# A planner that counts TensorE's instruction blocks, two products in other PSUM banks, and 25 stretches of the program with other priorities

## The chip, the cores and the metric

The kernel runs on one core of a Trainium2 chip. The metric is device time in microseconds (us) of one execution. Three runs of the kernel before gave 710.45 to 711.79 us, with a median of 711.58 us. One further execution was recorded by the hardware profiler, and all views below are of that one. Engines are named as the profile names them: PE is TensorE's matmuls, PEld its weight loads, DVE is VectorE, ACT is ScalarE, POOL is GpSimd, and SP is SyncE, which issues most DMAs.

## The reference

One layer of a decoder trunk over 512 tokens of width 1024, all in f32. Three groups of heads read the same normed input through one projection; their outputs are joined and go through one output projection; then comes a dense SwiGLU.

```python
h = rmsnorm(x, norm_mix[l])
mem_h = rmsnorm(mem, norm_mem[l])
proj = h @ w_in[l]
c_q, c_kv, k_rope, hq, hf, hi, hg, mq = [proj[..., offsets[j]:offsets[j + 1]] for j in range(len(IN_SIZES))]
y_mla = mla_group(c_q, c_kv, k_rope, positions, q_a_norm[l], w_uq[l], kv_a_norm[l], w_ukv[l],
                  mla_q_norm[l], mla_k_norm[l])
y_hg = hgrn2_group(hq, hf, hi, hg, lb_all[l], hg_out_norm[l])
y_mem = mem_group(mq, mem_h, w_mem_kv[l], mem_q_norm[l], mem_k_norm[l])
mix = jnp.concatenate([rmsnorm(y_mla, mla_out_norm[l]), y_hg, rmsnorm(y_mem, mem_out_norm[l])], axis=-1)
x = x + (mix @ w_out[l]).astype(x.dtype)
h2 = rmsnorm(x, norm_ffn[l])
x = x + ((jax.nn.silu(h2 @ w_gate[l]) * (h2 @ w_up[l])) @ w_down[l]).astype(x.dtype)
```

The first group is attention with low-rank q and kv, a rotary key and a causal softmax, the third is cross-attention into 256 memory tokens; each group has four heads. In the recurrence each head has q, k, v and a forget gate f per token: the state is multiplied by f, k's outer product with v is added, and q reads the state out.

## The kernel before, in words

**Arithmetic.** Nearly all products run on PE in the fp32r format. An f32 operand is split into a high part (`wh`, `xh`, `hd`: rounded by a copy) and a low part (`wl`, `xl`: source minus high part, on DVE), and `mm3` issues three matmuls, high by high, high by low and low by high, into one PSUM bank. `split`, `piece` and `pieces` make the two parts of a weight; `load` issues the weight's DMA on SP into a buffer `wr`.

**Planner.** `body` doesn't issue instructions. It calls a `Recorder`, which gives every operation a number in the order of the code (there are 5539), finds what it depends on, and gives it a price in ns (`price`) and a priority: its number plus a million times a class (0 for splits, evictions and loads, 1 as a rule, 2 for most projections). `base` adds two million from the FFN on. `run` then plays the five queues in time. At each step it takes, on the engine that can start first, the ready operation with the lowest priority number; an operation that needs a new tile waits until a buffer of that tag is free, and tiles of a tag are given out in the order of the code. Some operations may go to another engine than the code names when the planner finds them done sooner there (`others`). The order that comes out is issued as it stands, so each engine executes its part of it strictly in that order. The line numbers in the profile are therefore those of the two issuing lines: L383 for all operations, L380 for groups of small matmuls (`tiles`).

**PSUM.** There are eight banks under three tags: `mm` (3), `at` (3), `tr` (2). `gated` makes one 128-feature block of a projection: `feat` accumulates 8 x 3 matmuls into a bank, and DVE then multiplies it by `RX`, the per-token scale of the input's RMSNorm, into an SBUF tile `td`. `RX` exists only once the input's sums of squares are through. The first two blocks (i = 5 and i = 9: the first head's q and forget gate) have their weights under `in_we` and are multiplied chunk by chunk as `x` arrives. All blocks of `gated` take a bank `mm`.

**Stages, in the order of the code.** `hg_in`: eight blocks for the recurrence's q and f. `wide`: its values (weights `wva`, matmuls of 320 columns, and `wvb`, of 256 columns). `hg_levels`: inside chunks of 32 tokens, each level takes scores of all four heads by one `tiles` operation of 64 small f32 matmuls (32 x 32 columns; each becomes two passes, so 128 matmuls and 128 weight loads in the profile, `at<-y,tm`), DVE puts them in place under a mask (`put`, a copy_predicated), and `step_up` multiplies q, k and totals up to the next level, ten or more DVE operations. Then come `lowrank` (the compressed q and kv), the up projections (`wuq`, `wukv`), four heads of causal attention (`transposed`, `softmax`, `weights_t`, `pv`), the memory group, the output projection in two parts, and the FFN. The FFN runs in three column groups (`FF`), each with a gate and an up half made by `fast`, a scheme of seven block products (`prod`) instead of eight. `fast` loads weight blocks on SP (`get`) and adds further blocks onto them by accumulating DMAs on POOL (`more`), which must wait until the former content has been split. Each third ends with transposes of the activated product `ptl`, `p`, `qr`, `RX` and the `down` products.

**Price list.** The lines that the change touches: `price` for ACT (92 or 45 ns + 0.835 ns per element), for DVE's scalar_tensor_tensor (68 + 1.15 per element) and for DVE's other operations, copy_predicated among them (68 + 1.045). A `tiles` operation of 64 parts has the price 270 + 2.1 x 64 x 35 / 4 = 1446 ns, and nothing in the planner limits how soon the next one may follow.

Of the kernel before, what the change touches and what calls it, by code (L numbers as in the profile page):

```python
# [9 lines left out]
F32R = mybir.dt.float32r  # L10
I32 = mybir.dt.int32
U8 = mybir.dt.uint8
AF = mybir.ActivationFunctionType
# [33 lines left out]
class Recorder:  # L47
# [137 lines left out]
    def price(self, o, outs, ins):  # L185
        n = max(self._free(a) for a in outs)
        if o.name == "dma_start":
            return 1000 if o.eng == "gpsimd" else 475
        if o.eng == "tensor":
            if o.name == "tiles":  # L190
                return 270 + 2.1 * sum(max(35, self._free(p[2])) for p in o.kw["parts"]) / len({self._rng(p[0])[2] for p in o.kw["parts"]})
            if o.name == "transpose":
                return 109.5
            if ins[0].dtype == F32R:
                return n / 2.4 + (15.5 if n >= 512 else 14) if n >= 256 else max(1.67 * n, 107)
            return 222 if n <= 2 else 64 if n <= 32 else 122 if n <= 64 else 226 if n <= 128 else 436 if n <= 256 else 1.7 * n
        m = max([self._free(a) for a in ins] + [n])
        fast = self.inside(ins)
        if o.eng == "scalar":
            fn = o.args[2] if o.name == "activation" else None  # L200
            if fn is not None:
                o.table = self.TABLES.get(str(fn).split(".")[-1])
            return (92 if fast else 45) + 0.835 * m + (190 if "accum_out" in o.kw else 0) + (100 if hasattr(o.kw.get("scale"), "ap") else 0)
        if o.eng == "vector":
            if o.name == "reciprocal":
                return 70 + 6.6 * m
            if o.name == "tensor_copy":
                return 66 + (0.55 if fast else 1.045) * m
            if o.name == "tensor_scalar":
                return 66 + (0.62 if fast else 1.045) * m + 60 * any(hasattr(a, "ap") for a in o.args[2:])  # L210
            if o.name == "memset":
                return 60 + 0.5 * m
            if o.name == "scalar_tensor_tensor":
                return 68 + 1.15 * m
            return 68 + 1.045 * m
        if o.name == "memset":
            return 40 + m * 0.8
        if o.name == "tensor_scalar":
            return 244 + 0.84 * m
        return 170 + 2.17 * m  # L220
# [16 lines left out]
    }  # L237


    IDLE = (1500, 3400)  # L240

    def run(self):
        ops = self.ops
        for o in ops:
            o.left = len(o.preds)
            o.ready = 0.0
            for p in o.preds:
                ops[p].succs.append(o.n)
# [12 lines left out]
                    cand[e].append(o)  # L261
        table, dma, done, out, port, cold = None, 0.0, 0, [], 0.0, 0.0
        busy = {e: 0.0 for e in engs}
        while done < len(ops):
            best = None
            for e in engs:
                be = None
                for o in cand[e]:
                    t = max(free[e], o.ready)
                    if o.alts[e][5]:  # L270
                        t = max(t, port)
                    ok = True
                    if o.new:
                        need = {}
                        for k in o.new:
# [12 lines left out]
                            t = max(t, sorted(free_)[skip + j])  # L288
# [3 lines left out]
                    t = max(t, free[e])  # L292
# [33 lines left out]
            if o.eng == "tensor":  # L326
                if t - free["tensor"] > self.IDLE[0] or not free["tensor"]:
                    cold = t + self.IDLE[1]
                slow = min(2 * cost, max(0.0, cold - t))
                cost += slow / 2  # L330
            end = t + cost
            if both:
                port = end
# [2 lines left out]
            if o.dma:  # L336
                ap = o.kw["out"]
# [71 lines left out]
def body(ctx, tc, t):  # L409
# [14 lines left out]
    def nm(p):  # L424
        cnt[0] += 1
        return f"{p}_{cnt[0]}"
# [6 lines left out]
    def sb(tag, shape=(P, S), dt=F32):  # L433
        return rec.tile("SB", shape, dt, tag, nm(tag), BUFS[tag])

    def ps(tag, bufs, shape=(P, S)):
        return rec.tile("PS", shape, F32, tag, nm(tag), bufs)

    def ps_mm():
        return ps("mm", BUFS["mm"])  # L440

    def ps_at():
        return ps("at", BUFS["at"])

    def ps_tr():
        return ps("tr", BUFS["tr"])
# [28 lines left out]
    with rec.first(0):  # L475

        o = rec.tile("PS", (P, S), F32, "tr", nm("tr"), BUFS["tr"])
# [17 lines left out]
    def load(src, n=1024):  # L495

        raw = sb("wr", (P, 1024))
        with rec.first(0):
            DMA.dma_start(out=raw[:, :n], in_=src)
        return raw  # L500
# [43 lines left out]
    def colsums(sqs, nblk=NB, more=None):  # L544

        o = ps_ts()[:, 0:2 * nblk * len(sqs)]
        ks = [(i, b) for i in range(len(sqs)) for b in range(nblk)]
        v = o.rearrange("p (i b two) -> p i b two", two=2, b=nblk)
        T.tiles(o, ones, *sqs, parts=[
            (v[g:g + 32, i, b], sqs[i][:, b * P + g:b * P + g + 32], ones, (i, b) == ks[0], (i, b) == ks[-1] and more is None)  # L550
            for i, b in ks for g in range(0, P, 32)
        ])
        if more is not None:
            T.tiles(o, ones, more, parts=[
                (v[g:g + 32, 0, b], more[:, b * P + g:b * P + g + 32], ones, False, b == nblk - 1)
                for b in range(nblk) for g in range(0, P, 32)
            ])
        return v[..., 0]
# [27 lines left out]
    with rec.first(0):  # L586
# [6 lines left out]
        for k in range(KD):  # L593

            if k in EARLY:
                n, tag = EARLY[k]
# [9 lines left out]
        for k in range(KD):  # L606
            if k in EARLY:
                n = EARLY[k][0]
# [15 lines left out]
    def feat(dst, raw, acts):  # L624

        if isinstance(raw, list):
            w = raw.__getitem__
        else:
            w = pieces(raw)
        for k in range(KD):  # L630
            mm3(dst, w(k), acts[k], k == 0, k == KD - 1)
# [68 lines left out]

    def gated(i):

        o = ps_mm()
        feat(o, early[i // 9] if i in (5, 9) else load(t["wf"][i]), xg)
        z = sb("td")
        s_ = sb("td")
        with rec.first(0):
            V.tensor_tensor(z, o, RX, ALU.mult)
            A.activation(s_, z, AF.Sigmoid)
        return z, s_  # L710

    def hg_in(h):
        with rec.first(2):
            z, s_ = gated(5 + h)
            q = f(spots.pop(0))
            with rec.first(0):
                V.scalar_tensor_tensor(q, z, 128 ** -0.5, s_, ALU.mult, ALU.mult)
            z, s_ = gated(9 + h)
            fg = f(spots.pop(0))
            k_ = sb("tm")  # L720
            with rec.first(0):
                A.activation(fg, s_, AF.Identity, bias=lb[:, h:h + 1], scale=omlb[:, h:h + 1])
                A.activation(k_, fg, AF.Identity, bias=ones[:, 0:1], scale=-1.0)
                V.tensor_scalar(fg, fg, 1.0, None, ALU.min)
        return q, k_, fg
# [145 lines left out]
    def hg_gate(h, y):  # L871
        with rec.first(2):
            z, s_ = gated(13 + h)
        V.tensor_tensor(z, z, s_, ALU.mult)
        V.tensor_tensor(y, y, z, ALU.mult)
# [65 lines left out]
    with rec.first(0):  # L941
        o = colsums([cq_sq, ckv_sq])
# [25 lines left out]
    for h in range(4):  # L968
        o = ps_mm()
# [11 lines left out]
    for b in range(NB):  # L981
        o = ps_mm()[:, :256]
# [3 lines left out]
        o = o.rearrange("p (h d) -> p h d", h=4)  # L986
# [44 lines left out]
    for i in range(2):  # L1031
        w = [piece(r, i * S, (i + 1) * S) for r in wukv]
        for b in range(NB):
            o = ps_mm()
# [69 lines left out]
    def rope_t(src):  # L1104

        o = ps_tr()
        for b in range(NB):
            T.transpose(o[:, b * P:(b + 1) * P], src[:, b].rearrange("p a b -> p (a b)"), ident)
        return o

    ym = []
    for h in range(4):
# [6 lines left out]
        if h % 2 == 0:  # L1119
            o = rope_t(qr[:, :, h:h + 2, :])  # L1120
# [12 lines left out]
        for g in range(2):  # L1133
            pb = []
            for b in (2 * g, 2 * g + 1):
# [3 lines left out]
                o = ps_at()  # L1139
# [34 lines left out]
    for h in range(4):  # L1174
        o = ps_mm()
# [19 lines left out]
    for h in range(4):  # L1195
# [6 lines left out]
        for g in range(2):  # L1202
            pb = []
            for b in (2 * g, 2 * g + 1):
                bs = slice(b * P, (b + 1) * P)
                o = ps_at()
# [9 lines left out]
    with rec.first(2):  # L1216
        for i in range(KD):
            y = sb("tm")
            DMA.dma_start(out=y, in_=t["xT"][:, i * S:(i + 1) * S])
            o = ps_mm()  # L1220
# [12 lines left out]
    o = ps_tr()  # L1233
# [7 lines left out]
    for i in X_ORDER:  # L1241
        o = ps_mm()
# [54 lines left out]
    o = ps_tr()  # L1297
# [101 lines left out]
    for c0, w in FF:  # L1399
# [16 lines left out]
        for j in range(2 * w // P):  # L1416
            g, js = (cu[0:2] + cu[4:6], j * P) if j < w // P else (cu[2:4] + cu[6:8], j * P - w)
            hi, lo = sb("mx" if last else "xh", dt=F32R), sb("y" if last else "xl", dt=F32R)
            with rec.first(0):
                o = ps_tr()  # L1420
# [100 lines left out]
```

## Time and profile before

| what | value |
|---|---|
| median of three runs | 711.58 us (710.45 to 711.79) |
| the profiled execution's own time | 709.22 us |
| its span, first to last instruction | 707.4 us |
| instructions in the profile | 12975 |
| DVE busy | 546.7 us (77%) |
| ACT busy | 375.3 us (53%) |
| POOL busy | 92.8 us (13%) |
| moved by DMA | 98.04 MB, 139 GB/s on the mean |

The profiled execution lies 2.4 us below the median of the runs, and 1.8 us of it lie outside the span. PE's busy time counts matmuls whose starts are pipelined: a matmul of 512 columns is shown with some 0.39 us, while the next one starts some 0.23 us after it. What tells of lost time on PE is the idle time before an instruction, which the views print in square brackets with the instruction that ended it; "issue" there is a wait that nothing in the profile explains.

### The profile page before, as it was taken

How to read it: one execution, taken by the hardware profiler on the slowest of the kernel's cores; microseconds unless marked ns; L12 is line 12 of the kernel's file. 1: busy time of each engine (PE TensorE's matmuls, PEld its weight loads, DVE VectorE, ACT ScalarE, POOL GpSimd, SP SyncE). 2: the span in 40 equal slices, each digit the busy share in tenths (PEclk: the TensorE clock that was granted, in tenths of full speed). 3: DMA queues.
4: the chain of work that ended last, by engine and by line, in shares of the span. 5: the costliest groups of instructions: out<-in, count | busy, mean ns of one | idle time of the engine just before them, and what ended most of it. 6: DMA issues, size and time to landing. Idle time of an engine off the chain costs nothing.

```text
span 707.4 us, 12975 instructions
## 1 busy us (share of the span) xinstructions
PE 688.6 (97%) x4755; PEld 574.1 (81%) x4755; DVE 546.7 (77%) x1234; ACT 375.3 (53%) x721; POOL 92.8 (13%) x124
## 2 busy tenths in 40 slices
PE   8998899999999999999999998999999999999997
PEld 6787877887888877887878786888888899999886
DVE  7986799779989989888999769656549767548732
ACT  7763245447587654664776553645543365544420
POOL 1000000000000000000323442023112312310000
PEclk9999999999999999999999999999999999999999
DMA  8522221113333323215999899779957848941251
GB/s 284 161 66 91 84 63 46 31 63 120 89 120 120 118 65 101 75 31 183 281 278 226 182 244 218 191 164 219 212 127 184 162 130 193 225 87 34 68 146 62
DMA packets 47727, 98.04 MB, mean 139 GB/s; under 512 B 5424, under 2 KB 15536, under 8 KB 47664
## 3 DMA queue, kind: packets, MB, share of 16 engines
q1 hardware_dynamic: 33408, 73.62, 32.3%
q0 software_dynamic: 13824, 23.07, 20.4%
q8 instruction: 37, 0.61, 0.3%
q10 hardware_dynamic: 432, 0.53, 0.2%
q14 instruction: 26, 0.21, 0.1%
HBM read 95.11 MB, written 2.10 MB: 137 GB/s over the span
## 4 chain that ended last, share of the span: by engine, by line
PE 86%; DVE 6%; issue 3%; DMA 3%; ACT 2%; ACTq 0%; POOL 0%; DVEq 0%; POOLq 0%
PE mm L383 43%; PE tr L383 21%; PE at L383 20%; DMA xl<-in_wg 2%; DVE wl L383 2%; PE at L380 1%; DMA tc<-in_we 1%; DVE hd L383 1%; PE tr L380 1%; ACT wh L383 0%; DVE ptl L383 0%; DVE td L383 0%; DVE qr L383 0%; ACT hd L383 0%; DVE tm L383 0%
## 5 line engine op out<-in xcount | busy, mean ns | idle before, releaser
L383 ACT CAST wh<-wr 128x512 fp32r<-128x512 f32 (+2 forms) x141 | 84.0, 599 | 101.0 <-PE tr L383 44.4
L383 DVE TENSOR_TENSOR wl<-wr,wh 128x512 fp32r<-128x512 f32 (+2 forms) x148 | 96.9, 658 | 33.9 <-issue 11.6
L383 PE MATMUL mm<-xh,wh 128*128 128x512 f32 x248 | 98.0, 398 | 2.0 <-DVE td L383 1.5
L383 PE MATMUL mm<-xh,wl 128*128 128x512 f32 x248 | 98.4, 397 | 0.0
L383 PE MATMUL mm<-xl,wh 128*128 128x512 f32 x248 | 98.1, 396 | 0.1
L383 DVE TENSOR_TENSOR wl<-y,wh 128x512 fp32r<-128x512 f32 (+1 forms) x84 | 53.4, 638 | 41.8 <-PE tr L383 19.3
L383 ACT CAST wh<-y 128x512 fp32r<-128x512 f32 (+1 forms) x82 | 47.4, 581 | 65.9 <-PE at L383 35.5
L383 DVE TENSOR_TENSOR wl<-mx,wh 128x512 fp32r<-128x512 f32 (+1 forms) x72 | 46.1, 645 | 33.5 <-PE tr L383 14.8
L383 PE MATMUL mm<-wh,hd 128*128 128x512 f32 (+2 forms) x176 | 59.7, 366 | 0.7 <-ACT wh L383 0.7
L383 ACT CAST wh<-mx 128x512 fp32r<-128x512 f32 (+1 forms) x67 | 39.0, 585 | 37.2 <-PE at L383 17.7
L383 PEld LDWEIGHTS mm<-xh,wh 128*128 128x128 f32 x248 | 46.6, 188 | 11.5 <-DVE td L383 1.8
L383 PEld LDWEIGHTS mm<-xl,wh 128*128 128x128 f32 x248 | 46.6, 188 | 9.9 <-DVE xl L383 1.0
L383 PEld LDWEIGHTS mm<-xh,wl 128*128 128x128 f32 x248 | 46.7, 188 | 9.0 <-DVE wl L383 0.4
L383 POOL DMA_DIRECT2D y<-in_wu x36 | 32.2, 955 | 104.4 <-DVE wl L383 77.2
L383 PE MATMUL at<-wh,hd 128*128 128x512 f32 (+1 forms) x120 | 45.0, 375 | 0.0
L383 PE MATMUL tr<-xl,wh 128*128 128x512 f32 x112 | 43.8, 391 | 0.0
L383 PE MATMUL tr<-xh,wl 128*128 128x512 f32 x112 | 43.7, 390 | 0.0
L383 PE MATMUL tr<-xh,wh 128*128 128x512 f32 x112 | 43.7, 390 | 0.0
L383 PEld LDWEIGHTS mm<-wh,hd 128*128 128x128 f32 x176 | 32.3, 188 | 5.8 <-ACT wh L383 1.1
L383 PE MATMUL mm<-wh,v 128*128 128x512 f32 (+1 forms) x96 | 35.8, 375 | 0.0
L383 PE MATMUL at<-wh,v 128*128 128x512 f32 (+1 forms) x96 | 35.8, 375 | 0.0
L383 PE MATMUL mm<-wl,hd 128*128 128x512 f32 (+2 forms) x88 | 32.5, 369 | 0.4 <-DVE wl L383 0.4
(409 smaller groups left out, 1676.9 us busy)
## 6 DMA issues: line engine op xcount, KB each, us to landing
wr<-in_wf SPq DMA_DIRECT2D x19, 512.0 KB, 3.4
wr<-in_wd SPq DMA_DIRECT2D x16, 512.0 KB, 4.7
mx<-in_wg SPq DMA_DIRECT2D x24, 256.0 KB, 5.4
mx<-in_wu SPq DMA_DIRECT2D x24, 256.0 KB, 5.7
y<-in_wu POOLq DMA_DIRECT2D x24, 256.0 KB, 6.3
tm<-in_xT SPq DMA_DIRECT2D x16, 256.0 KB, 4.5
wr<-in_wt SPq DMA_DIRECT2D x8, 512.0 KB, 3.8
wr<-in_wo SPq DMA_DIRECT2D x8, 512.0 KB, 3.6
```

What stands on the lines that cost most here:

```text
L380: r = self.nc.tensor.matmul(get(a), lhsT=get(b), rhs=get(c), start=first, stop=last, skip_group_check=True)
L383: r = getattr(getattr(self.nc, o.eng), o.name)(*[get(a) for a in o.args], **{k: get(a) for k, a in o.kw.items()})
```

## The change

It has three parts, all in the plan or in tile tags; no operation is added or taken away.

1. **Prices and a count of blocks in the planner.** ACT activations of the kind Identity cost 90 ns more, scalar_tensor_tensor with a tile as its scalar 35 ns more, copy_predicated 118 in place of 68 ns. New: `length` gives PE operations a number of instructions (2 for a transpose or an fp32r matmul, 4 for an f32 matmul, 4 per part of a `tiles` operation). `run` counts these, starting from 63, and at each multiple of 256 it does not let the new block begin earlier than 5200 ns after the one before; what is missing is added to the operation's price.
2. **Other banks for two products.** In `gated`, blocks 5 and 9 take a bank `at` and no longer a bank `mm`.
3. **25 stretches get other priorities.** `NUDGE` holds triples (first, last + 1, shift): the shift is added to the priority of these operations. A positive shift puts them behind more of the others that are ready.

Where the stretches lie, by operation number (counted in the order of the code):

| operations and shift | what they are |
|---|---|
| 381-384 +76, 415-437 +197, 447-450 +346, 448-451 -155, 526-527 +71 | `wide`: matmuls of `wva` and `wvb`, and the splits of one weight piece |
| 606-649 +233, 617-638 -329 | last value splits; the first four `tiles` operations of `hg_levels` and their DVE steps |
| 791-800 +36 | `lowrank`: matmuls of the first block |
| 1159-1170 +125, 1280-1281 +16 | `wuq` and `wukv` products |
| 1871-1917 -113 | end of the last causal head; first memory weights with 2 loads on SP |
| 2480-2481 +413, 2552-2576 -90, 2651-2672 +978, 2666-2678 -114 | output projection, first part: blocks with 2 loads on SP each |
| 2912-2915 -11, 2923-2937 +28 | FFN input: differences and splits |
| 3042-3061 +1406, 3078-3080 +75 | first gate half: products 1 and 5 with their splits |
| 3321-3355 -51, 3385-3478 +368, 3440-3442 -146, 3549-3551 +692 | first up half: products 5, 7, 6, 2, 4; 4 loads on SP, 8 on POOL |
| 3588-3685 -133 | first third's transposes; second gate half's loads (12 on SP, 12 on POOL) and first product |
| 5484-5497 +129 | `down` of the last third: one load, one output DMA, splits, matmuls |

```diff
@@ price
-            return (92 if fast else 45) + 0.835 * m + (190 if "accum_out" in o.kw else 0) + (100 if hasattr(o.kw.get("scale"), "ap") else 0)
+            return (92 if fast else 45) + 0.835 * m + 90 * (fn == AF.Identity) + (190 if "accum_out" in o.kw else 0) + (100 if hasattr(o.kw.get("scale"), "ap") else 0)
...
             if o.name == "scalar_tensor_tensor":
-                return 68 + 1.15 * m
+                return 68 + 1.15 * m + 35 * hasattr(o.args[2], "ap")
+            if o.name == "copy_predicated":
+                return 118 + 1.045 * m
             return 68 + 1.045 * m
@@ class Recorder
+    FETCH, BLOCK, AHEAD = 5200, 256, 63
+
+    def length(self, o):
+
+        if o.name == "tiles":
+            return 4 * len(o.kw["parts"])
+        return 2 if o.name == "transpose" or o.kw["rhs"].dtype == F32R else 4
...
+    NUDGE = ((1159, 1171, 125), (1871, 1918, -113), (2651, 2673, 978), (2666, 2679, -114), (2552, 2577, -90), (3042, 3062, 1406), (5484, 5498, 129), (2480, 2482, 413), (1280, 1282, 16), (526, 528, 71), (2912, 2916, -11), (3588, 3686, -133), (2923, 2938, 28), (3385, 3479, 368), (3078, 3081, 75), (3321, 3356, -51), (791, 801, 36), (3549, 3552, 692), (381, 385, 76), (3440, 3443, -146), (617, 639, -329), (415, 438, 197), (447, 451, 346), (448, 452, -155), (606, 650, 233),)
 
     def run(self):
         ops = self.ops
+        for a, b, d in self.NUDGE:
+            for o in ops[a:b]:
+                o.prio += d
...
         busy = {e: 0.0 for e in engs}
+        begun, count = -1e9, self.AHEAD
...
                 slow = min(2 * cost, max(0.0, cold - t))
                 cost += slow / 2
+                n, full = self.length(o), cost
+                count += n
+                for b in range((count - n) // self.BLOCK + 1, count // self.BLOCK + 1):
+                    at = t + cost - full * (count - self.BLOCK * b) / n
+                    cost += max(0.0, begun + self.FETCH - at)
+                    begun = max(at, begun + self.FETCH)
@@ gated
-        o = ps_mm()
+        o = ps_at() if i in (5, 9) else ps_mm()
         feat(o, early[i // 9] if i in (5, 9) else load(t["wf"][i]), xg)
```

## Prediction

> **What bounds the kernel now.** I read the page first: which engine is busy, at what clock, and who holds the chain that ended last.
>
> ```profile
> PE 688.6 (97%) x4755; PEld 574.1 (81%) x4755; DVE 546.7 (77%) x1234; ACT 375.3 (53%) x721; POOL 92.8 (13%) x124
> PEclk9999999999999999999999999999999999999999
> PE 86%; DVE 6%; issue 3%; DMA 3%; ACT 2%; ACTq 0%; POOL 0%; DVEq 0%; POOLq 0%
> ```
>
> PE is busy 97% of the span, at full clock in all slices, and holds 86% of the chain. The change neither adds nor removes a matmul, so it can gain only what PE idles, and it loses by any idle time that the new order brings. The second view is therefore PE's list of waits, which has 13 rows; here are the larger ones and the last.
>
> ```profile
> PE at L380 <- issue: 4.5, 2, 2.9
> PE tr L383 <- DVE ones_r L383: 2.0, 1, 2.0
> PE tr L383 <- DVE ptl L383: 2.0, 2, 1.7
> PE mm L383 <- DVE td L383: 1.5, 1, 1.5
> PE at L380 <- DVE tm L383: 1.1, 2, 0.8
> PE mm L383 <- ACT wh L383: 0.7, 1, 0.7
> PE mm L383 <- DVE wl L383: 0.7, 3, 0.3
> PE mm L383 <- ACT xh L383: 0.5, 2, 0.3
> ...
> PE tr L383 <- DVE kr L383: 0.2, 1, 0.2
> ```
>
> The columns are the total, the number of waits and the longest. The rows shown make 13.2 us; the four left out hold 0.3 or 0.4 us each, 1.4 us in sum. Of the whole, 14.6 us, the 2.0 us for `ones_r` lie before the first matmul and the 0.5 us for `xh` in the arrival of the input, which no part of the change touches. About **12.1 us** are all that a better order could gain: 1.7% of the time.
>
> **Part 2 of the change: banks for the first two blocks.** The timeline around 25 us (start, duration, instruction, idle time before it):
>
> ```profile
> 19.20 0.40 PE L383 MATMUL mm<-xh,wh 128*128 128x512 f32 x1
> 19.43 0.39 PE L383 MATMUL mm<-xl,wh 128*128 128x512 f32 x1
> ...
> 24.73 0.47 PE L383 MATMUL mm<-xh,wl 128*128 128x512 f32 x1
> 25.06 0.58 ACT L383 COPY RX<-tr 128x512 f32<-128x512 f32 x1
> 25.92 1.28 DVE L383 TENSOR_TENSOR td<-mm,RX 128x512 f32<-128x512 f32 x2
> 26.66 0.50 PE L383 MATMUL mm<-xh,wh 128*128 128x512 f32 x1 [1.46 <-DVE td L383]
> ```
>
> Blocks 5, 9 and the third one hold all three `mm` banks, and `RX` is ready only at 25.64, so the fourth block waits until DVE has drained the first bank. With blocks 5 and 9 in `at` banks, the fourth and fifth block find two `mm` banks free. What could be late next is the sixth block, two blocks of 24 matmuls later (24 x 0.23, the step between the first two rows, is 5.5 us each), by when the third bank is drained. The `at` banks are next wanted by the first score operation past 58 us. Bounds: nothing, if the fourth block's split weights are not ready (DVE makes one at 25.31 to 26.00), and 1.7 us with the refilling of the pipeline. I take **-1.5**, the row of the wait.
>
> **Part 1: blocks of instructions.** The wait "issue" of 4.5 us comes twice, both times inside a score operation:
>
> ```profile
> 60.64 0.86 PE L380 MATMUL at<-y,tm 128*32 128x32 f32 x76
> 64.39 0.65 PE L380 MATMUL at<-y,tm 128*32 128x32 f32 x52 [2.89 <-issue]
> 80.37 1.13 PE L380 MATMUL at<-y,tm 128*32 128x32 f32 x108
> 83.09 0.38 PE L380 MATMUL at<-y,tm 128*32 128x32 f32 x20 [1.59 <-issue]
> 88.27 1.30 PE L380 MATMUL at<-y,tm 128*32 128x32 f32 x128
> ```
>
> An undisturbed one (the last row) runs 128 matmuls and as many loads in 1.30 us. The page's queue list and the window from the stall's beginning to its end say what is fetched in that time:
>
> ```profile
> q8 instruction: 37, 0.61, 0.3%
> ...
> q8 instruction: 1, 0.02, 2.1%
> ```
>
> PE has 2 x 4755 = 9510 instructions; 9510 / 256 = 37.1, and queue 8 brought 37 packets: blocks of 256 instructions, one of which lands in the first stall. Counting 256 back from the second stall gives the pace that the chip keeps:
>
> ```profile
> 77.90:81.49 3.59, 3.59 (x129) 3.30 (x127) 2.44 (x7) 0.62 (x1) 0.00 (x0) 1.00 0.47 151
> ```
>
> 129 matmuls and 127 loads took 3.59 us, and with the stall of 1.59 they make 5.18 us. Before the first stall 256 instructions reach back to about 59.2 us: 2.3 us and 2.89 make again 5.2. So a block takes at least 5.2 us; the planner's new FETCH is this number, and its boundary can be checked by it. A score operation is itself 256 instructions in 1.3 us, and stalls when most of one falls into one block; where a boundary cuts it in the middle (the one at 88.27) the rest of the block, some 64 wide matmuls, lasts longer than 5.2 us by itself. The planner only has to move these operations by some matmuls of `wide`, which are there in plenty, and the first seven stretches do this. Bounds: nothing gained, if the count is off, and -4.5. I take **-4.2**, near the upper end, and leave 0.15 us each time.
>
> The Trainium skill (page "Runtime: NRT & Kernel Launch", section "Instruction fetch mechanics") also has refills in blocks of 256 instructions, but calls the cost of crossing a block mostly hidden and the fetch faster than PE's dispatch. By that rule the stalls would be something else and the term 0, the forecast 4.2 us higher. The two stalls above, with a block landing in the first, speak against it.
>
> **The scores' other waits.** The rest of the waits of score operations are on DVE's steps between levels.
>
> ```profile
> L380 PE MATMUL at<-y,tm 128*32 128x32 f32 x704 | 7.9, 198 | 5.3 <-issue 4.5 <-DVE tm L383 0.8
> 58.00:88.00 30.00, 25.29 (x654) 23.82 (x653) 22.52 (x59) 7.41 (x15) 0.00 (x0) 1.00 0.25 80
> 88.00:124.00 36.00, 34.53 (x509) 27.95 (x509) 33.28 (x105) 17.68 (x42) 0.00 (x0) 1.00 0.18 58
> L383 DVE COPY_PREDICATED tc<-lmask,at 128x512 f32<-128x512 uint8 x5 | 3.7, 740 | 7.4 <-PE at L380 7.4
> ```
>
> In the two windows the columns are PE, PEld, DVE, ACT and POOL busy. From 88 to 124 us PE idles 1.5 us and DVE only 2.7, so a chain of levels that starts later has little room; from 58 to 88 DVE idles 7.5 us. A copy_predicated takes 740 ns; the old price for 512 elements is 603, the new one 653: nearer, not there. The dearer Identity and scalar_tensor_tensor only correct the plan in the same sense and move no work that the trace shows waiting; I cost them at nothing. Of the waits here (1.1 us on `tm` in the list) I take half, **-0.6**; bounds -1.1 and +2.7, the latter if a delayed chain eats DVE's slack and PE pays as much again.
>
> **The FFN's first third.** Its largest wait is for the activated product:
>
> ```profile
> 436.20 0.39 PE L383 MATMUL at<-wh,hd 128*128 128x512 f32 x1
> 436.31 0.70 DVE L383 TENSOR_TENSOR ptl<-mm,ptl 128x512 f32<-128x512 f32 x1
> 437.51 1.42 DVE L383 SCALAR_TENSOR_TENSOR ptl<-ptl,r,tc 128x512 f32<-128x512 f32 x2
> 438.32 0.44 PE L383 MATMUL tr<-cst,ptl 128*128 128x128 f32 x2 [1.74 <-DVE ptl L383]
> ...
> 380.00:400.00 20.00, 19.79 (x115) 15.18 (x115) 19.22 (x42) 13.06 (x21) 5.75 (x7) 1.00 0.91 201
> 400.00:420.00 20.00, 20.00 (x89) 16.27 (x88) 11.81 (x20) 11.03 (x21) 4.39 (x6) 1.00 1.04 251
> 420.00:440.00 20.00, 17.45 (x76) 12.91 (x76) 19.08 (x31) 6.78 (x12) 8.03 (x10) 1.00 1.03 232
> ```
>
> DVE idles 8.2 us between 400 and 420 and 0.9 us in the next 20, where PE idles 2.6; ACT idles 13.2 us there. The last products end, and four DVE operations stand between them and the transposes, while the next third's weights queue for the same DVE. The stretches from 3042 to 3685 reorder these products, splits and loads; the same work fits without the wait if a product or splits move ahead. PE's waits here are `ptl` 2.0, `wh` 0.7 and `wl` 0.7, in sum 3.4. I take **-2.1**, some six tenths, since four DVE operations at the end remain in series; bounds -3.4 and +1.5 (DVE is full from 380 to 400, too).
>
> **The other stretches** (`lowrank`, `wuq`, attention, output projection, `down`) lie where PE's waits are 0.2 to 0.4 us each. I take 0, bounds -1 and +1. The loads moved there are 7 on SP and one output DMA. They are the cheapest to hide:
>
> ```profile
> SPq L383 <- DVE wl L383: 543.5, 162, 22.8
> y<-in_wu POOLq DMA_DIRECT2D x24, 256.0 KB, 6.3
> POOL y L383 <- DVE wl L383: 129.4, 29, 20.1
> ```
>
> SP spends 543.5 us in waits for DVE to release a buffer: buffers, not SP's order, set when loads start, so a load moved within SP's queue still goes out when a `wl` is done. The accumulating loads on POOL (20 moved, with 16 of SP, in the FFN stretches) also wait for DVE, and land 6.3 us after issue; two products of 24 matmuls, 11 us, hide that today.
>
> **Sum.** -1.5 - 4.2 - 0.6 - 2.1 = -8.4 us. The profiled execution would come from 709.22 to 700.8. The median of the runs is 2.36 us above that execution; the prediction is for the median: 711.58 - 8.4 = **703.2 us**, with its own range from 701 to 706.
>
> **Rivals.**
> *Everything goes.* The reordering also fills the small waits: 711.58 - 12.1 = 699.5 us. For it: the waits are spread over stages with stretches in them. Against it: DVE is full around most of them.
> *The count misses.* The planner's boundary lies elsewhere than the chip's (PE's own semaphore instructions are not in its count), or the stalls have another cause than blocks, and they stay or move to another score operation: 703.2 + 4.2 = 707.4 us. For it: 76 and 108 matmuls into an operation, a shift of some 50 matmuls decides. Against it: 9510 / 256 gives the 37 packets, so few instructions are uncounted, and two stalls of different length give one pace, 5.2 us. The Trainium skill's rule named above would lead to this time as well.
> *Late weights in the FFN: slower.* The up half's stretch +368 puts 4 SP and 4 POOL loads behind later products, and the stretch -133 draws 12 and 12 of the next gate half into the middle of them. If an accumulating load is issued only when its product is next, PE stands for its landing and the two steps of its split, 6.3 + 0.7 + 0.7 = 7.7 us (each step taken as long as the DVE operation at 436.31). One such load leaves the kernel 0.7 us faster; from two on it is slower: 711.58 - 8.4 + 15.4 = 718.6 us. Against it: today no accumulating load shows in PE's waits, and 11 us of products lie between.
>
> **How the numbers follow.** Forecast 0.56, everything goes 0.13, the count misses 0.21, late weights 0.10 (0.06 with two or more, 0.04 with one). About 0.2%, 1.4 us, is what a measurement of this kernel can tell from no change. Faster by more has the first two cases and nearly all of the third (707.4 is 4.2 below before), 0.88; one late load gives most of "same", 0.06; slower 0.06. The range for 8 in 10: down to 699.5, where everything goes; up to 708.8, the third case with 1.4 us of the unknown bounds on top.
>
> **What would show it.** The wait "issue" of L380 gone from PE's list, and score operations cut by block boundaries; no wait for `td` near 25 us; the wait for `ptl` near 436 below 1 us; DVE less idle between 400 and 420. Wrong would be: a DMA as the releaser of a PE wait in the FFN, a longer wait for `tm` between 88 and 124, or a stall "issue" at another place.

## The result and the profile after

The changed kernel takes **699.15 us** (median of 4 runs, 698.81 to 699.73); beside it the kernel before took 711.68 us (4 runs, 710.45 to 712.3). The ratio is 0.9826, with an interval of 0.9811 to 0.9842: 12.5 us faster. The forecast was 8.4 us and 703.2 us; the result lies just below the range, whose low end was 699.5.

The page of the changed kernel, the lines that answer to those of before:

```profile
PE 688.4 (99%) x4755; PEld 575.6 (83%) x4755; DVE 549.4 (79%) x1231; ACT 375.9 (54%) x723; POOL 93.8 (13%) x127
PEclk9999999999999999999999999999999999999999
PE 89%; DVE 8%; ACT 1%; issue 1%; DVEq 0%; ACTq 0%
```

PE's work is the same to 0.2 us; its idle time went. The complete list of PE's waits in the changed kernel (total, number, longest; the issuing lines 380 and 383 are now 405 and 408):

```profile
PE tr L408 <- DVE ones_r L408: 2.0, 1, 2.0
PE at L408 <- DVE tm L408: 0.6, 2, 0.4
PE tr L408 <- ACT tm L408: 0.6, 1, 0.6
PE at L405 <- DVE tm L408: 0.4, 1, 0.4
PE mm L408 <- DVE wl L408: 0.4, 2, 0.2
PE at L408 <- ACT p L408: 0.2, 1, 0.2
PE at L408 <- ACT tc L408: 0.2, 1, 0.2
```

The sum is 4.4 us against 14.6 before. "issue", `td`, `ptl` and `wh` are gone, and no DMA has come in as a releaser. The windows say in which stage the time was won. The columns are the length of the window, then the busy time of PE, PEld, DVE, ACT and POOL, PE's granted clock, the DMA share and GB/s. First the kernel before, then the changed one:

```profile
10.00:50.00 40.00, 38.49 (x199) 30.70 (x198) 37.10 (x97) 30.98 (x51) 0.00 (x0) 1.00 0.48 159
50.00:100.00 50.00, 45.29 (x1021) 41.30 (x1020) 38.98 (x106) 16.30 (x34) 0.00 (x0) 1.00 0.24 76
100.00:300.00 200.00, 197.33 (x1543) 161.82 (x1542) 177.68 (x494) 119.40 (x257) 4.38 (x16) 1.00 0.27 86
300.00:500.00 200.00, 196.53 (x978) 157.97 (x977) 162.33 (x312) 115.39 (x210) 52.24 (x61) 1.00 0.82 203
```

```profile
10.00:50.00 40.00, 39.98 (x208) 32.45 (x207) 37.99 (x99) 33.87 (x55) 0.00 (x0) 1.00 0.49 160
50.00:100.00 50.00, 49.37 (x1101) 44.77 (x1100) 43.38 (x122) 21.09 (x43) 0.00 (x0) 1.00 0.28 84
100.00:300.00 200.00, 198.17 (x1503) 161.34 (x1489) 175.79 (x482) 117.56 (x260) 6.39 (x20) 1.00 0.27 84
300.00:500.00 200.00, 199.64 (x995) 162.38 (x994) 168.08 (x314) 116.26 (x205) 53.61 (x62) 1.00 0.88 213
```

The first number less the second is PE's idle time: 1.5, 4.7, 2.7 and 3.5 us before, 0.0, 0.6, 1.8 and 0.4 after. So 1.5 us were won at the banks, 4.1 from 50 to 100 us, where most of the scores lie, 0.8 from 100 to 300 us and 3.1 in the last window, most of it in the FFN; with 0.5 us in the first 10 us, this is the 9.9 us by which the span became shorter (707.4 to 697.5). Cut at 125 us, the 0.8 us fall to the last scores: PE idles 1.5 us from 100 to 125 before and 0.5 after, and from 125 to 300 us 1.2 before and 1.3 after. The medians differ by 12.5. Some **2.5 us** of the gain stand in neither of these two profiles, and this is what the prediction missed most.

### The profile page after: what moved, and what is told of

It reads as the page before. It is cut to its first block, busy times and chain, and to the rows that moved or that the text cites. A ratio compares the mean times of both kernels' runs of the same rounds, so it can differ in the third digit from the quotient of the medians.

```text
span 697.5 us, 13013 instructions
## 1 busy us (share of the span) xinstructions
PE 688.4 (99%) x4755; PEld 575.6 (83%) x4755; DVE 549.4 (79%) x1231; ACT 375.9 (54%) x723; POOL 93.8 (13%) x127
## 4 chain that ended last, share of the span: by engine, by line
PE 89%; DVE 8%; ACT 1%; issue 1%; DVEq 0%; ACTq 0%
PE mm L408 43%; PE at L408 23%; PE tr L408 22%; DVE wl L408 2%; DVE tm L408 1%; DVE hd L408 1%; PE at L405 1%; DVE y L408 1%; DVE td L408 1%; DVE tc L408 1%; PE tr L405 1%; ACT wh L408 0%; DVE qr L408 0%; DVE sm L408 0%; ACT td L408 0%
## 5 line engine op out<-in xcount | busy, mean ns | idle before, releaser
L408 ACT CAST wh<-wr 128x512 fp32r<-128x512 f32 (+2 forms) x139 | 82.3, 595 | 85.7 <-PE mm L408 40.3
L408 PE MATMUL mm<-xh,wh 128*128 128x512 f32 x232 | 91.5, 396 | 0.0
L408 PE MATMUL mm<-xl,wh 128*128 128x512 f32 x232 | 91.4, 397 | 0.0
L408 PE MATMUL mm<-xh,wl 128*128 128x512 f32 x232 | 90.6, 395 | 0.2 <-DVE wl L408 0.2
L408 PEld LDWEIGHTS mm<-xh,wl 128*128 128x128 f32 x232 | 43.6, 188 | 8.7 <-DVE wl L408 0.6
L408 PEld LDWEIGHTS mm<-xh,wh 128*128 128x128 f32 x232 | 43.6, 188 | 8.4 <-ACT wh L408 0.2
L408 PEld LDWEIGHTS mm<-xl,wh 128*128 128x128 f32 x232 | 43.5, 188 | 8.3 <-DVE xl L408 0.2
```

Source lines behind the costliest of these rows:

```text
L408: r = getattr(getattr(self.nc, o.eng), o.name)(*[get(a) for a in o.args], **{k: get(a) for k, a in o.kw.items()})
```

## The experiments

The theory at first was the prediction's: counting blocks keeps the scores apart, and the stretches of the FFN take its wait away. The rival: the order comes from the stretches alone, wherever they lie. Four kernels leave out stretches from the changed kernel; prices, count and banks stay. No kernel has the prices alone.

**All stretches out.**

```diff
-    NUDGE = ((1159, 1171, 125), (1871, 1918, -113), (2651, 2673, 978), ...
+    NUDGE = ()
```

> The changed kernel without its 25 stretches: banks, prices and the count of blocks stay. Theory A (the prediction's): the count by itself makes the planner hold the score operations apart, so the two stalls 'issue' (4.5 us) and the wait for RX (1.5 us) go and the FFN's waits (3.4 us) stay: about 6 us below before, 705 to 707 us. Theory B: the planner takes the first ready operation and the count only tells it that it will have to wait; then stalls 'issue' of 4 us or more stay in the list of waits, only the 1.5 us of the banks is gained, and the time is 709 to 713 us.

Measured: 706.78 us (7 runs, 705.19 to 708.73), ratio 0.9935 (0.9912 to 0.9958). From PE's waits:

```profile
PE at L405 <- issue: 3.2, 1, 3.2
PE tr L408 <- DVE ptl L408: 2.4, 2, 2.2
...
PE at L405 <- DVE tm L408: 1.1, 2, 0.8
```

The time alone would speak for theory A, the list speaks for B as to the first stall: the count is in this kernel's plan, and a stall of 3.2 us remains. The planner only adds the missing time to the price of an operation: it sees the stall and pays it, since it always takes what can start first. The second stall is gone without any stretch, and the banks are not the reason, since the kernel with the banks alone (below) still has it. What is left is the count or the prices. The planner can be played through without the chip: with the count and the old prices it gives PE the order of the kernel before, past both stalls; with the new prices and no count it gives the order of this kernel there. So the order that goes with the loss of the second stall comes from the prices. This is computed, not measured.

**Groups of stretches out.** `no_early` drops the seven below operation 700, `no_mid` those from 791 to 2678, `no_late` those from 2912 on.

> The changed kernel without the seven stretches below operation 700 (values projection and scores). Theory A: as the changed kernel, 699 to 700 us, for the count does the work there. Theory B: stalls 'issue' return, 4 to 5 us, 703 to 705 us, while the FFN's wait for ptl stays away.

> The changed kernel without the stretches from 791 to 2678 (low-rank, attention, output projection). Prediction's view: they lie where PE waits little, so within 1 us of the changed kernel. Rival: they decide when the FFN's loads and splits start, or where blocks of instructions fall near 150 us, and 3 us or more come back as PE waits (ptl, or issue).

> The changed kernel without the stretches from 2912 on (FFN). Prediction's view: the FFN's waits of 3.4 us come back (ptl near 436 us of before, wh, wl), 702 to 703 us. Rival: the FFN's waits were set by how the stage is entered, and the time stays within 1.4 us of the changed kernel's 699.15.

Measured: without the early ones 703.89 us (701.82 to 704.34), ratio 0.9892 (0.9867 to 0.9916); without the middle ones 704.49 us (703.96 to 705.13), 0.9905 (0.9884 to 0.9927); without the late ones 700.15 us (700.04 to 700.43), 0.9844 (0.9819 to 0.987). The three single losses, 4.7, 5.3 and 1.0 us, make more than the 7.6 us of all together. Half-clock time, of which below, is in the first two and in the 7.6; but in the executions whose mean clock was nearest to full (0.999 without the early ones and with all out, 1.000 for the other two) the losses are 2.7, 4.9 and 1.0 us against 6.6 together, so the groups do not simply add.

PE's matmuls around 58 us without the early stretches (start, duration, instruction, idle time before it), then the same place in the changed kernel:

```profile
57.98 0.46 PE L405 MATMUL at<-ptl,tm 128*32 128x32 f32 x32
59.14 0.86 PE L405 MATMUL at<-y,tm 128*32 128x32 f32 x76
62.71 0.96 PE L405 MATMUL at<-y,tm 128*32 128x32 f32 x52 [2.70 <-issue]
```

```profile
57.18 0.46 PE L405 MATMUL at<-ptl,tm 128*32 128x32 f32 x32
57.56 0.42 PE L408 MATMUL tr<-wl,xh 128*128 128x320 f32 x1
...
60.74 0.31 PE L408 MATMUL tr<-wl,xh 128*128 128x320 f32 x1
60.98 1.30 PE L405 MATMUL at<-y,tm 128*32 128x32 f32 x128
```

Two `tiles` operations of 256 instructions follow each other here. Without the early stretches the second begins 0.7 us after the end of the first; in the changed kernel 22 matmuls of `wide` with 320 columns lie between them, 3.3 us, where the kernel before has 5. So the early stretches took the first stall away. Without the middle stretches nothing shows as "issue"; the largest waits are these:

```profile
PE mm L408 <- DVE wl L408: 1.9, 3, 1.4
PE mm L408 <- DVE qr L408: 1.2, 1, 1.2
PE at L405 <- DVE tm L408: 1.0, 2, 0.7
PE tr L408 <- DVE xl L408: 0.8, 1, 0.8
```

PE then idles 4.0 us between 300 and 500 us: 1.4 us near 388, 1.6 us near 429, where the first third ends, and 0.8 us near 452. Without the late stretches it idles 1.4 us there, against 0.4 us in the changed kernel. The wait for `ptl` itself comes back in none of the three kernels, only with all stretches out (2.4 us); without the middle ones waits for `qr` and `wl` stand in its place. So with the other stretches in, those between the scores and the FFN are worth 3.6 us of idle time here, and those that reorder the FFN's own products, to which the prediction gave it, 1.0 us.

**The count taken out, the stretches left in.**

```diff
-    FETCH, BLOCK, AHEAD = 5200, 256, 63
+    FETCH, BLOCK, AHEAD = 0, 256, 63
```

> The changed kernel with all stretches, banks and prices, but the least time of a block set from 5200 ns to 0, so that the planner no longer sees blocks. Theory 'the stretches carry the gain': they keep the score operations apart without the count, stalls 'issue' of at most 1 us, 699 to 701 us. Theory 'count and stretches belong together': the priorities then meet another plan, stalls of 2 us or more return, 702 to 706 us.

Measured: 699.39 us (699.01 to 700.05), ratio 0.9836 (0.9808 to 0.9863), no wait "issue". PE's order is the changed kernel's, instruction by instruction. With the stretches in place the count gives nothing; it may have served to choose them, which no run here can tell.

**The banks alone.** The kernel before with its order on every queue, blocks 5 and 9 in `at` banks:

```diff
+        if i in (5, 9):
+            swap.append(o.tensor.name)
...
+    for k in swap:
+        rec.tiles[k][0] = "at"
```

> The kernel before with its old plan and order; only the two first products of gated lie in at banks. Prediction's term: the wait for td near 25 us goes, 1.5 us less, 709.5 to 710.5 us where before gives its usual 711.6. Rival: the 1.5 us come back as longer waits for DVE between 58 and 124 us, since DVE and ACT start the scores' inputs no earlier; within 0.5 us of before.

Measured: 709.25 us (12 runs, 706.75 to 711.51), ratio 0.9962 (0.9941 to 0.9982). The wait for `td` has left the list; "issue" is 4.0 us, the 0.5 us for `xh` are not there, and the others stand within 0.1 us of before. Of the runs at a mean granted clock of 1.000, the five of this kernel lie at 706.75 to 708.11 us, the four of the kernel before beside it at 709.15 to 709.63, on the mean 2.1 us more. The term of 1.5 us is shown by the list; the rest goes with the shorter first stall.

**All instructions further on in their blocks.** Six of the ten warm-up matmuls at the start are replaced by 54 of 32 x 32, so that all later PE instructions lie 96 places further on; order and results stay. Once in the kernel before, once in the changed one:

```diff
+                if warm > 4:
+                    for i in range(9):
+                        x, y = get(o.args[0])[:32, 0, :32], o.kw["lhsT"][:, :32]
+                        r = self.nc.tensor.matmul(x, lhsT=y, rhs=y, start=True, stop=True)
...
+                    continue
```

> The kernel before in its own order; of its ten warm-up matmuls six are replaced by 54 of 32 x 32, which puts all that follows 96 PE instructions further on in the blocks of 256. Theory 'blocks' (the chip brings PE's instructions in blocks of 256, and a block lasts at least some 5.2 us): the stalls 'issue' move; counted in the trace of before, the first comes some 30 matmuls earlier in the second score operation (near 61 us, 3.1 us), the one at 81.5 us goes, and new ones come near 71 us (4.0 us) and 95 us (1.7 us); in sum 8 to 9 us in place of 4.5, and 714 to 718 us. Theory 'operation' (the stall belongs to the score operations themselves): 2.9 and 1.6 us at the old places, time as before.

> The changed kernel in its own order, moved by the same 96 instructions. Theory 'blocks': its order keeps clear of stalls only for the place of the boundaries that the planner counted; moved, some 5 to 8 us of stalls 'issue' come back, the largest near 89 us (3.6 us) and others near 65 and 71 us, 704 to 709 us. Theory 'operation', or 'scores that stand apart never stall': no stall, 699 to 700 us.

Measured: 710.82 us (10 runs, 707.52 to 713.34), ratio 0.9986 (0.9963 to 1.001), and 701.53 us (4 runs, 700.86 to 701.85), ratio 0.9857 (0.9829 to 0.9885). In the shifted kernel before:

```profile
63.94 1.05 PE L389 MATMUL at<-y,tm 128*32 128x32 f32 x100 [1.52 <-issue]
69.22 1.30 PE L389 MATMUL at<-y,tm 128*32 128x32 f32 x128
71.40 0.30 PE L392 MATMUL mm<-wh,xh 128*128 128x320 f32 x1 [0.88 <-issue]
```

The first stall now comes after 28 matmuls of its operation, not after 76: 48 matmuls and 48 loads earlier, the 96 instructions of the shift. The one near 81 us is gone, another has appeared behind a score operation. So block boundaries are the places of the stalls. In sum there are 2.4 us of them, where 8 to 9 were expected. Their length is not what the prediction's pace gives: from 69.22 to 71.40 a whole operation of 256 instructions and its stall took 2.2 us, not 5.2. In the changed kernel I expected stalls to return; 0.5 us did. Part of its other 2 us is the clock at the start, which with the smaller warm-ups stayed low until 11.6 us, where it had risen at 7.9.

**What makes a block late.** In the kernel before, the packet of the block that the first stall waits for began 2.9 us after PE had entered the block before it, while a weight load of 512 KB (the second `wvb`) was landing. One kernel holds this load back on SP by a one-column copy on POOL until 62.8 us; another adds four unread loads of 256 KB right behind it.

```diff
+                r = self.nc.gpsimd.tensor_copy(x[:, 0:1], get(o.args[0])[:, 0, 0, 0:1])
...
+                r = self.nc.sync.dma_start(out=x, in_=held.kw["in_"])
```

```diff
+                    for j in range(4):
+                        x = pools["SB"].tile([P, S], F32, tag="hd", name=f"more{j}", bufs=10)
+                        r = self.nc.sync.dma_start(out=x, in_=self.more[j])
```

> The kernel before in its own order; only the second wvb weight load (issued at 58.6 us, 512 KB, in flight during the first stall) is held on SP until DVE has read out the first scores, some 61 us, by a copy of one column on POOL that the load must follow. Theory 'contention': the block of instructions is late because its packet queues behind the load's (it starts 2.9 us after the boundary, where undisturbed ones start 1.0 to 1.2 us after it); without the load it starts at about 60.3 us, and the first stall falls from 2.9 to about 1 us; the second stays near 1.6. Theory 'pace' (5.2 us per block whatever else runs): 2.9 and 1.6 us as before.

> The kernel before in its own order, with four further loads of 256 KB (1 MB that nothing reads) on SP right behind the second wvb load. Theory 'contention': 64 KB more on each of 16 DMA engines, at the 0.95 us that a 16 KB packet of instructions takes some 3.9 us, so the first stall grows from 2.9 to between 5 and 7 us. Theory 'pace': it stays at 2.9 us.

Measured: 709.72 us (10 runs, 707.49 to 712.31), ratio 0.9979 (0.9957 to 1.0), and 712.41 us (10 runs, 710.58 to 713.9), ratio 1.0017 (1.0001 to 1.0034). The first stall with the load held, then with loads added:

```profile
62.73 0.65 PE L386 MATMUL at<-y,tm 128*32 128x32 f32 x52 [0.88 <-issue]
```

```profile
65.02 0.96 PE L381 MATMUL at<-y,tm 128*32 128x32 f32 x52 [3.24 <-issue]
```

Against 2.89 us before, holding the load takes 2.0 us away: the packet now begins 0.85 us after the boundary, lands 1.0 us later, and PE goes on 1.4 us after that. The second stall, whose load was not held, is still 1.9 us. Adding loads behind brings only 0.35 us, where I had expected 2 us and more: what counts seems to be what is already moving when the block is asked for.

**Where the other 2.5 us are.** The kernel before once more, unchanged, for a second profile:

> The kernel before once more, for a second profile. The runs of before spread from 709.2 to 714.2 us, with a mean granted clock of 1.000 to 0.993, those of the changed kernel from 698.8 to 699.7 at 1.000. Theory 'clock': a run above 710 us shows one to three stretches of 3.4 us at half clock right after a stall, each worth 1.2 to 1.7 us, and the same waits as the first profile. Rival: no such stretch, but longer waits for DMA or DVE.

Measured: 713.32 us, span 711.5 us, with the list of waits of the first profile (15.1 us in sum against 14.6). The windows, with PE's clock third from the end:

```profile
66.69:70.10 3.41, 3.41 (x15) 3.41 (x14) 2.66 (x9) 0.62 (x1) 0.00 (x0) 0.50 0.00 0
442.10:445.50 3.40, 3.40 (x10) 2.83 (x11) 2.95 (x5) 1.37 (x4) 2.28 (x3) 0.51 0.50 70
```

PE ran at half clock for 3.4 us in two places, one after the first stall "issue" and one after the wait for `ptl`. Two such stretches at half speed cost up to 3.4 us; the span is 4.1 us longer than in the first profile, whose mean clock was 1.000, and 0.5 us of it are waits. Over all 67 runs of the kernel before that were made beside the experiments, sorted by their mean granted clock:

| mean clock | runs | time, us |
|---|---|---|
| 1.000 | 14 | 708.44 to 709.63 |
| 0.998 | 19 | 709.48 to 711.39 |
| 0.995 | 20 | 711.52 to 713.13 |
| 0.993 | 13 | 712.95 to 714.67 |
| 0.990 | 1 | 716.25 |

One stretch of 3.4 us lowers the mean by 1.7 / 709 = 0.0024, one step of the table, and costs some 1.5 us. The four runs of the changed kernel beside its result are all at 1.000. But the two kernels differ in much else, so a stall was put into the changed kernel with nothing moved: ahead of a `down` product near 669 us PE waits for an ACT copy and POOL memsets that its own tiny matmul sets off.

```diff
+            if o.n == 5392:
...
+                self.tc.keep_in_program_order(self.nc.scalar.copy(x[:32, :32], y[:32, :32]))
+                for j in range(2):
+                    self.tc.keep_in_program_order(self.nc.gpsimd.memset(x[:, :], 1.0))
+                self.tc.keep_in_program_order(self.nc.tensor.matmul(y[:32, :32], lhsT=x[:32, :32], rhs=x[:32, :32], start=True, stop=True))
```

> The changed kernel with one pause of PE near 660 us, at the start of a down product: a tiny matmul, an ACT copy, two POOL memsets of 128x512 (0.53 us each in the changed kernel's rows) and a tiny matmul that reads them; PE stands for about 0.8 + 2 x 0.53 = 1.9 us. The result is unchanged. If half clock follows from a stall: some executions show a mean clock of 0.997 to 0.999 and are up to 1.7 us longer than the others, 701.1 to 702.8 us. If half clock has another cause that the changed kernel happens to lack: all executions stay at 1.000 and within 1 us, at 701.1 us.

> The same with four memsets: PE stands for about 2.9 us, as long as the first stall of the kernel before. If half clock follows from a stall: more of the executions than with the short pause have a clock below 1.000, and the times are 702.1 us without and 703.8 us with a half-clock stretch of 3.4 us. If it has another cause: 702.1 us throughout, at 1.000.

> The same with eight memsets: PE stands for about 5.0 us, longer than 3.4. If half clock follows from a stall: every execution has a half-clock stretch of at least 3.4 us, 704.2 + 1.7 = 705.9 us or more. If it has another cause: 704.2 us, at 1.000.

| memsets | pause, us | runs at clock 1.000, us | runs below it, us |
|---|---|---|---|
| none | none | 698.81, 699.06, 699.25, 699.73 | none |
| 2 | 1.6 | 701.04, 701.20 | 703.39, 703.41 (0.998) |
| 4 | 2.7 | 702.65, 702.95 | 703.92, 704.06 (0.997) |
| 8 | 5.0 | none | 705.97 to 707.38 (ten runs: nine 0.995, one 0.997) |

The ratios to the kernel before are 0.9871 (0.9812 to 0.9929), 0.9892 (0.9844 to 0.994) and 0.994 (0.9919 to 0.9961). PE's list has the pause of the short kernel, and its windows a half-clock stretch right behind (the next one is back at 0.98):

```profile
PE tr L416 <- POOL pause L415: 1.6, 1, 1.6
```

```profile
671.90:675.50 3.60, 3.60 (x11) 2.81 (x10) 0.29 (x1) 0.40 (x1) 0.00 (x0) 0.54 0.28 106
675.50:679.00 3.50, 3.50 (x17) 2.91 (x16) 1.43 (x3) 0.62 (x1) 0.00 (x0) 0.98 0.20 33
```

With 512 columns PE did 11 matmuls in 3.6 us there, where it does 16 or 17 in such a time at full clock. The long pause has two half-clock stretches in a row:

```profile
671.90:675.40 3.50, 1.68 (x5) 1.34 (x6) 0.00 (x0) 0.00 (x0) 1.59 (x4) 0.50 0.13 50
675.40:678.80 3.40, 3.40 (x10) 2.65 (x9) 0.00 (x0) 0.00 (x0) 0.00 (x0) 0.51 0.02 5
678.80:682.00 3.20, 3.20 (x16) 2.65 (x15) 1.72 (x3) 1.03 (x2) 0.00 (x0) 1.00 0.00 0
```

A stall alone brings the half clock: of 1.6 and 2.7 us in two of four runs each, of 5.0 us in all ten. The kernel before has four waits of 1.5 us and more on which this can follow (2.9 and 1.6 us for blocks, 1.7 for `ptl`, 1.5 for `td`); in the changed kernel the longest behind its first matmul is 0.6 us. This settles the 2.5 us: they are half-clock time, which went with the stalls.

**When a stall brings half clock.** The traces also say what the chance in this table is. In each of the 16 traces, all changes of the granted clock lie whole multiples of 3.41 us apart (in the second profile of before 18, 1, 109, 1 and 78 of them). So each execution can be cut into windows of 3.41 us that begin where its clock first rose. This table sorts the windows at full clock of all traces by PE's idle time in them:

| PE idle in the window, us | windows | next window at half clock |
|---|---|---|
| 1.79 to 3.24 | 11 | 11 |
| 1.55 to 1.75 | 9 | 2 |
| up to 1.53 | 3203 | 0 |

About half a window of idle time decides, whatever caused it, and a stall that falls into two windows counts in parts. A half-clock window was followed by another only twice, after 1.80 and 1.44 us of idle time in it. Two windows of the middle pause, then two of the short one:

```profile
666.91:670.32 3.41, 1.89 (x10) 1.23 (x8) 1.72 (x3) 1.10 (x3) 1.05 (x2) 1.00 0.55 170
670.32:673.74 3.42, 2.23 (x11) 1.85 (x12) 0.00 (x0) 0.00 (x0) 1.05 (x2) 1.00 0.54 182
```

```profile
668.80:672.21 3.41, 1.86 (x11) 1.45 (x11) 1.03 (x2) 0.59 (x2) 1.05 (x2) 1.00 0.49 120
672.21:675.62 3.41, 3.41 (x10) 2.67 (x9) 0.41 (x1) 0.40 (x1) 0.00 (x0) 0.50 0.21 77
```

The profiled run with the pause of 2.7 us had it cut into 1.53 and 1.19 us and kept its clock; the pause of 1.6 us lay in one window and cost a half-clock one. The first profile of before had windows with 1.75, 1.74 and 1.59 us of idle time and escaped narrowly. In the changed kernel no window after the clock's rise has more than 0.6 us, wherever the windows fall.

## Why the prediction was right and wrong

**The carry-over to the median** is the step that failed. The text took the 2.36 us between the profiled execution and the median as an offset that stays, and gave no reason. They are half-clock stretches behind waits that the change removes; the profiled execution, at clock 1.000, was one of the fifth of executions (14 of 67) that had none. At equal clock the gain is 709.2 - 699.15 = 10.0 us, and the rest up to 12.5 is this. It makes 2.4 of the 4.05 us by which the forecast was too high. The hint stood in the kernel: in its plan `run` doubles PE's prices for 3.4 us behind an idle time of more than 1.5 us (`IDLE = (1500, 3400)`).

**The banks**, -1.5: right, by the list of waits and by the kernel with the banks alone; no sixth block came late.

**The blocks**, -4.2: right in size (4.5 went). Two parts of its reasoning fell. The pace of 5.2 us is not the chip's own: both stalls of before had a weight load in flight, and two equal numbers under the same condition were read as a constant. And the count does not move the score operations. The early stretches do it for the first stall, as the text also said; the second went without them, with the order that the new prices make (as far as computed), two of which the prediction put at nothing because they move no work that waits. The rival that the count misses had its danger in the wrong place: with the stretches the order depends little on where a boundary lies, as far as one shift by 96 instructions with 0.5 us of stall shows.

The Trainium skill (page "Runtime: NRT & Kernel Launch", section "Instruction fetch mechanics"), which calls the crossing of a block mostly hidden, holds here for blocks of wide matmuls (every wait "issue" in the lists stands in a score operation or at most 2.3 us behind one) and not for 256 instructions that PE finishes in 1.3 us.

**The scores' other waits**, -0.6: the wait of `at` for `tm` in line 405 fell from 1.1 to 0.4 us, and the waits of the same kind in line 408 took 0.3 of it back. Right in kind, 0.2 us too much.

**The FFN**, -2.1: it was -3.1 by the windows and -3.0 by the list (`ptl`, `wh` and `wl`: 3.4 us before, 0.4 after). The caution, that four DVE operations at the end stay in series, did not hold: they are now spread from 427.95 to 432.36 us, the transposes come in two pairs, at 430.77 and 432.84, and products of PE lie between. The cause was put in the wrong stretches: without those of the FFN all but 1.0 us of the time is still won, without the middle ones PE idles 4.0 us there. Which stretch does it was not taken apart further.

**The other stretches**, 0: right by the windows, since PE's idle time from 125 to 300 us is 1.2 us before and 1.3 after. But 0 is not what they are worth: without the middle ones the time is 4.9 us longer at full clock, as said of the FFN. The 0.5 us for `xh` in the first 10 us are no effect of the change: this wait is 1.0 us in the second profile of before and 0.5 again in the kernel without the count.

**The rivals.** "Everything goes" came nearest, with 699.5 us, though not by its own account: 9.7 of its 12.1 us went (2.4 are left without `ones_r`), and the half-clock time made up for the rest. For "late weights" nothing is seen, no DMA releases a PE wait. The terms taken from waits were together 1.6 us too small, and 703.2 - 1.6 = 701.6 would have lain in the forecast's own range; the offset would have had to be seen as a cost of the stalls.

## What to carry to other kernels

Before a gain in one profiled execution is carried over to a median, compare the mean granted clock of the two: where executions of a kernel differ in steps of some 1.5 us, price PE's stalls with their idle time and, where they can add up to 1.5 us and more within 3.4 us, with a chance of half-clock time behind them. A group of hundreds of small matmuls runs through an instruction block faster than the next one comes; put wide matmuls between two such groups, and keep large loads from starting just ahead of them. A planner that prices a stall does not thereby avoid it: look whether the order changes.

## What the runs showed of the hardware

- **Half clock after short stalls.** Stalls of 1.6 and 2.7 us brought a half-clock stretch of about 3.4 us in two of four runs, one of 5.0 us two stretches in the profiled run; so did one of 3.2 us, with all stretches out. The Trainium skill (page "TensorE: Matmul & The Clock Gate", section "Part 1: The HAM clock gate (the "warmup" mystery)") has the clock fall to half after at least one idle window of some 3.4 us, with windows that run on freely. The grid of 3.41 us in the traces agrees; that a whole window must be idle does not. From full clock, all 11 windows with 1.79 us of idle time and more were followed by half clock, 2 of 9 with 1.55 to 1.75 us, none of 3203 with less.
- **Instruction blocks behind a load.** The packet of a block began 0.85 us after the boundary with no load in flight, and 2.9 us after it with 512 KB landing; 1 MB more queued behind that load added 0.35 us to the stall. A late packet need not cost: counted on from the first stall of the kernel before, PE crossed a boundary of 256 instructions at 423 us, in the FFN; the packet began 26 us later, PE was 29 us in that block, and no "issue" shows at its end.
